# A two-layer decoder trunk in split fp32r: the tokens' high and low parts as one 512-column product

## The chip, the cores and the metric

The kernel runs on one core of a Trainium2 chip. The metric is the device time of one execution in microseconds. A kernel is timed in several runs and the median is given. One more execution is taken by the hardware profiler: it gives the page, the chain of waits and the timeline that are quoted here.

## The reference

Two pre-norm residual layers on 256 tokens of width 2048, all in float32. Layer a is multi-head latent attention, layer b block-sparse attention, which with 256 tokens is plain causal attention with ALiBi. Each has 16 heads of width 128, and a gate path that multiplies what the mixer gives before the output projection.

```
def moba_mixer(h, w_in, q_norm, k_norm):
    q, k, v, gate = jnp.split(h @ w_in, 4, axis=-1)
    q = rms_norm(to_heads(q, N_HEADS, HEAD_DIM), q_norm)
    k = rms_norm(to_heads(k, N_HEADS, HEAD_DIM), k_norm)
    v = to_heads(v, N_HEADS, HEAD_DIM)
    o = moba_attention(q, k, v, alibi_slopes())
    return from_heads(o) * jax.nn.silu(gate)

def reference(x, ...):
    for i in range(DEPTH):                       # DEPTH = 2
        if i == 0: y = mla_mixer(rms_norm(x, norm_a[0]), ...) @ w_out_a[0]
        if i == 1: y = moba_mixer(rms_norm(x, norm_b[0]), ...) @ w_out_b[0]
        x = x + y
    return x
```

In layer b, w_in is 2048 x 8192 (q, k, v and gate, 2048 columns each), w_out is 2048 x 2048.

## The kernel before

**Split products.** float32 data is cut into a high part in fp32r and a low part (what is left of it, again fp32r), and a product is the sum of three: high x high, high x low, low x high. Tokens are held with the features on the partitions: xh and xl are [128, 16, 256] (16 row blocks of 128 features, 256 tokens), ogh and ogl the same for the gated outputs of the 16 heads.

**Weights.** A weight piece is 128 x 1024 values (512 KB): SyncE's queue loads it (wr, four buffers, L132), ACT casts its high part (wh, four buffers, L146) and DVE subtracts to make the low part (wl, three buffers, L150). `run` issues these ahead of the step that uses the piece. A buffer is free again when TensorE is done with its piece.

**Blocks.** `blk_rows` has the weights stream as 512 moving columns against the tokens (q, k and v). `blk_cols` has the tokens stream as 256 moving columns against 128 weight columns, three products of 256 columns for each row block and each 128 weight columns (gates and output blocks). Two such 256-column results share a PSUM bank, five banks hold accumulators (`acc`).

**Order.** Each block is a list of steps, one for each row block. `ordered` sets one order of all steps by hand-written costs and lags: main steps in their list's order, side steps (attention heads, token scales) where their inputs are reckoned to be ready. TensorE's instructions are chained in that order. The other engines take their rows in an order of their own, fixed when the program is built.

**A head** has three side steps (`head_steps`): s1 makes the scores in PSUM (ps_s) and the softmax (sm: minimum on DVE, exp on ACT, normalising on DVE); s2 turns the probabilities by a DMA transpose, with a DVE copy out to pz in front (L407), the transpose issued by SyncE (L408) and a DVE copy back behind it (L409), and cuts them into ph (ACT), pl (DVE) and p1; s3 makes the product with v (ps_o), multiplies by the gate (og) and splits into ogh and ogl. Output block steps need the ogh and ogl of their head: step 12 that of head 12, and so on.

**Layer b** goes in four groups of four heads. A group is its gate block, q, k and v; the heads of a group run under the next group's gate, those of the last group under the first output blocks (`outs_b`). `gate_done` multiplies a gate by the token scale rows (rr) and applies tanh; `token_scale` makes these rows from ps_st and ps_r.

Of the kernel before, what the change touches and what calls it, by code (L numbers as in the profile page):

```python
# [21 lines left out]
F32R = mybir.dt.float32r  # L22
# [4 lines left out]
ALU = mybir.AluOpType  # L27

P = 128
S = 256  # L30
DM = 2048
NC = DM // P
H = 16
# [43 lines left out]
def paired(v):  # L77

    return v.rearrange("p (g l e) -> p g e l", l=2, e=16)


def lines(v):

    return v.rearrange("p (g l e) -> p g l e", l=2, e=16)


def unpaired(v):

    return v.rearrange("p (g e l) -> p g l e", l=2, e=16)
# [3 lines left out]
def trunk(ctx: ExitStack, tc, xT, gains, cst, w_in_a, w_q_up, w_kv_up, w_out_a, w_in_b, w_out_b, outT):  # L93
    nc = tc.nc
    pool = lambda name, **kw: ctx.enter_context(tc.tile_pool(name=name, **kw))
    one = pool("one", bufs=1)
# [5 lines left out]
    def acc(name):  # L102
        return pacc.tile([P, 512], F32, tag="acc", name=name)
# [86 lines left out]
    def chain(ins):  # L190

        if pe:
            tc.add_manual_dep(ins.ins, pe[-1].name, mybir.DependencyInfo(
                mybir.DependencyClass.NoSync, mybir.DependencyReason.DATA), reason="order")
        pe.append(ins.ins)

    def matmul(*args, **kw):
        chain(nc.tensor.matmul(*args, skip_group_check=True, **kw))  # L198
# [4 lines left out]
    def blk_rows(w, x, done, lag=PB, first=()):  # L203

        nk, n = w.shape[0] // P, w.shape[1]
        a = []

        def go(wt, c, k):
            xh, xl = x()
            if k == 0:  # L210
                a.extend(acc("acc") for _ in range(2))
            for t in range(2):
                ts = slice(t * P, (t + 1) * P)
                o = a[t][:, :n]
                matmul(o, xh[:, k, ts], paired(wt.h[:, c]), start=k == 0, stop=False)
                matmul(o, xh[:, k, ts], paired(wt.l[:, c]), start=False, stop=False)
                matmul(o, xl[:, k, ts], paired(wt.h[:, c]), start=False, stop=k == nk - 1)
            if k == nk - 1:
                done([a[t][:, :n] for t in range(2)])

        return _steps(w, go, 6 * (n / 2.4 + 2.5), lag, first, True)

    def blk_cols(w, x, done, lag=3000):

        nk, ns = w.shape[0] // P, w.shape[1] // P
        a = []

        def go(wt, c, k):
            xh, xl = x()
            if k == 0:  # L230
                a.extend(acc("acc") for _ in range(ns // 2))
            for s in range(ns):
                o = a[s // 2][:, (s % 2) * S:(s % 2 + 1) * S]
                ws = slice(s * P, (s + 1) * P)
                first = k == 0 and s % 2 == 0
                last = k == nk - 1
                matmul(o, wt.h[:, c, ws], paired(xh[:, k]), start=first, stop=False)
                matmul(o, wt.h[:, c, ws], paired(xl[:, k]), start=False, stop=False)
                matmul(o, wt.l[:, c, ws], paired(xh[:, k]), start=False, stop=last)
            if k == nk - 1:  # L240
                done(a)

        return _steps(w, go, 3 * ns * 109, lag)

    def _steps(w, go, cost, lag, first=(), moving=False):
        out, nc_w = [], 1024 // w.shape[1]
        nk = w.shape[0] // P
        k1 = 0
        for n in list(first) + [nc_w] * nk:
            k0, k1 = k1, min(k1 + n, nk)  # L250
            if k0 == nk:
                break
            wt = W(w[k0 * P:k1 * P], moving)
            for k in range(k0, k1):
                out.append(Step(lambda wt=wt, c=k - k0, k=k: go(wt, c, k), cost, lag if k == nk - 1 else 0,
                                w=wt if k == k0 else None))
        return out
# [26 lines left out]
    def big(dtype=F32):  # L284
        return one.tile([P, NC, S], dtype, tag="xt", name="xt")

    res["x"] = big()
    xh = one.tile([P, NC, S], F32R, name="xh")
    xl = one.tile([P, NC, S], F32R, name="xl")
    ogh = one.tile([P, H, S], F32R, name="ogh")  # L290
    ogl = one.tile([P, H, S], F32R, name="ogl")
    ident = c_sb[:, C_ID:C_ID + P]
    ones = one.tile([P, P], F32, name="ones")
    nc.vector.memset(ones, 1.0)
# [16 lines left out]
    def split_x(c, gcol):  # L311
        xt = res["x"]
        res["split"] = nc.scalar.activation(xh[:, c], xt[:, c], AF.Copy, scale=col(gcol + c))
        nc.vector.scalar_tensor_tensor(xl[:, c], xt[:, c], col(gcol + c), xh[:, c].bitcast(F32),
                                       op0=ALU.mult, op1=ALU.subtract)
# [6 lines left out]
    def sum_squares(ssq, j):  # L322

        xt = res["x"]
        sq = wk.tile([P, 2, S], F32, tag="gx", name="sq")
        after(nc.scalar.activation(sq, xt[:, 2 * j:2 * j + 2], AF.Square), res["split"])
        if j == 0:
            nc.vector.tensor_tensor(ssq, sq[:, 0], sq[:, 1], op=ALU.add)
        else:
            nc.vector.tensor_tensor(ssq, ssq, sq[:, 0], op=ALU.add)  # L330
            nc.vector.tensor_tensor(ssq, ssq, sq[:, 1], op=ALU.add)
# [26 lines left out]

    gate_of = {}

    def gate_done(g, rows):
        def done(a):
            for b in range(len(a)):
                ub = wk.tile([P, 2, S], F32, tag="gate", name="gate", bufs=4)
                gate_of[g + b] = ub
                x = wk.tile([P, 2, S], F32, tag="gx", name="gx")
                nc.vector.tensor_tensor(x, a[b].rearrange("p (h t) -> p h t", h=2),
                                        rows().unsqueeze(1).to_broadcast([P, 2, S]), op=ALU.mult)
                nc.scalar.activation(ub, x, AF.Tanh, scale=0.5)
                nc.vector.scalar_tensor_tensor(ub, ub, 1.0, x, op0=ALU.add, op1=ALU.mult)  # L370
        return done


    def products(ps, q, k, first):
# [87 lines left out]
    main, side = [], []  # L462
# [122 lines left out]
                transpose(ps[:, i * S + t * P:i * S + (t + 1) * P], src.rearrange("p a b -> p (a b)"), ident)  # L585
        parts(ps, 1.0, krf, *lat_st["kr"], True)

    x_a = lambda: (xh, xl)
    rows_a = lambda: scale_a["rows"]
    lat0 = blk_rows(w_in_a[:, 0:LAT // 2], x_a, lat_acc.append, 0, (1, 1))  # L590
    lat1 = blk_rows(w_in_a[:, LAT // 2:LAT], x_a, lat_acc.append, 0)
# [123 lines left out]
    def out_done_a(j):  # L715
        def f(a):
            xt = res["x"]
            c = 2 * j
            both = lines(xt[:, c:c + 2].rearrange("p a b -> p (a b)"))
            nc.vector.tensor_tensor(both, unpaired(a[0]), both, op=ALU.add)  # L720
            split_x(c, G_NB)
            split_x(c + 1, G_NB)
            sum_squares(ssq_b, j)
        return f
# [5 lines left out]
    ssq_b = one.tile([P, S], F32, tag="ssq", name="ssq")  # L730
    scale_b = {}
    rx2 = one.tile([P, 2], F32, name="rx2")
    og = lambda: (ogh, ogl)
    outs_a = [blk_cols(w_out_a[:, 256 * j:256 * (j + 1)], og, out_done_a(j), 4000) for j in range(8)]

    for g in range(8):
        main += group_a(g)
# [20 lines left out]
    x_b = x_a  # L758
    rows_b = lambda: scale_b["rows"]

    def group_b(g):
        z = {}
# [59 lines left out]
            return f  # L822

        w = lambda i: w_in_b[:, DM * i + 512 * g:DM * i + 512 * (g + 1)]
        gate = blk_cols(w(3), x_b, gate_done(2 * g, rows_b))
        q = blk_rows(w(0), x_b, n_done("q"))
        k = blk_rows(w(1), x_b, n_done("k"))
        v = blk_rows(w(2), x_b, v_done, 3000)
        old = hb[4 * g - 8:4 * g - 4] if g > 1 else []
        last = [h[0] for h in hb[-4:]] if g else [h[0] for h in heads[-4:]]  # L830
        tq = Step(turn("q", gq_b), 0, TUB, q[-1:], last)
        tk = Step(turn("k", col(G_KB)), 0, TUB, k[-1:], last)
        for h in range(4):
            hb.append(head_steps(4 * g + h, scores(h), bias(4 * g + h), lambda h=h: [x[:, h] for x in z["v"]],
                                 545, [tq, tk], v[-1:] + gate[-1:], [], S2B, nc.vector.tensor_copy))
        gate[-1].after += [h[2] for h in old] + [row_b]
        v[-1].after += [h[2] for h in old]
        if g:
            q[-1].after += turns_of[-2]
            k[-1].after += turns_of[-1]  # L840
        else:
            for i, s in enumerate(gate):
                s.needs.append(outs_a[i // 2][-1])
        turns_of.extend([[tq], [tk]])
        side.extend([tq, tk])
        side.extend(s for h in hb[-4:] for s in h)
# [2 lines left out]
    def out_done_b(j):  # L849
        def f(a):  # L850
            xt = res["x"]
            for b in range(2):
                c = 4 * j + 2 * b
                y = xt[:, c:c + 2]
                both = lines(y.rearrange("p a b -> p (a b)"))
                nc.vector.tensor_tensor(both, unpaired(a[b]), both, op=ALU.add)  # L856
                nc.sync.dma_start(outT[c * P:(c + 2) * P].rearrange("(c p) t -> p c t", p=P), y)
        return f

    outs_b = [blk_cols(w_out_b[:, 512 * j:512 * (j + 1)], og, out_done_b(j)) for j in range(4)]  # L860

    col_b, row_b = token_scale(ssq_b, "b", scale_b, [outs_a[7][-1]], scales_b)
    side += [col_b, row_b]
    hb = []
    for g in range(4):
        main += group_b(g)
    for b in outs_b:
        for i, s in enumerate(b):
            s.needs.append(hb[i][2])
    main += outs_b[0][:12] + outs_b[1][:6] + outs_b[0][12:] + outs_b[1][6:] + outs_b[2] + outs_b[3]  # L870
    run(ordered(main, side))


# [59 lines left out]
```

## Time and profile before

| | us |
|---|---|
| median of 3 runs | 759.71 (758.45 to 760.53) |
| profiled execution, whole time | 760.14 |
| its span | 758.0 |
| TensorE busy in it | 746.2 (98%) |
| weight loads busy | 708.0 (93%) |
| DVE busy | 576.2 (76%) |
| ACT busy | 488.3 (64%) |

PE is TensorE's products, PEld its weight loads, DVE the vector engine, ACT the scalar engine, SPq the queue of SyncE, which issues the DMAs. A product's recorded duration contains its way through the array, so products overlap in the records; the pace is read from their starts. "x12" is a count of instructions.

### The profile page before, as it was taken

The page shows a single profiled execution, that of the slowest core. Times are in us where ns is not written, and L with a number is a line of the kernel's source. Part 1 is how long each engine was busy: PE and PEld are TensorE (multiplying, and loading weights), DVE is VectorE, ACT ScalarE, POOL GpSimd, SP SyncE. Part 2 cuts the span into 40 slices and gives each one's busy share as a digit, 9 for nine tenths or more (in the row PEclk, how much of TensorE's full clock was granted, in tenths as well). Part 3 has the DMA queues.
Part 4 walks back from the last instruction along what each step waited for, and adds up shares of the span by engine and source line. Part 5 has one row for each costly group of instructions (what it writes and reads, how often), then busy time and mean ns, then how long its engine had stood idle before and what let it go on. Part 6 is the DMA issues. An engine that isn't in the chain of part 4 may idle for free.

```text
span 758.0 us, 14123 instructions
## 1 busy us (share of the span) xinstructions
PE 746.2 (98%) x5246; PEld 708.0 (93%) x5246; DVE 576.2 (76%) x1207; ACT 488.3 (64%) x1025; POOL 0.2 (0%) x4
## 2 busy tenths in 40 slices
PE   8999999999999899999999999999999999999997
PEld 7999999999999899998889988998889988899997
DVE  6888899898997585765888767886688857887552
ACT  7767888888877464545667566665567666574431
POOL 0000000000000000000000000000000000000000
PEclk9999999999999999999999999999999999999999
DMA  9866665666557966667886778876788778867771
GB/s 304 257 177 180 185 177 167 181 156 185 162 167 222 248 195 199 196 189 202 228 234 174 200 221 229 229 188 208 188 240 230 188 211 220 231 181 215 250 223 44
DMA packets 137973, 153.19 MB, mean 202 GB/s; under 512 B 47280, under 2 KB 94768, under 8 KB 137904
## 3 DMA queue, kind: packets, MB, share of 16 engines
q1 hardware_dynamic: 137760, 152.27, 70.7%
q8 instruction: 41, 0.67, 0.4%
q14 instruction: 28, 0.23, 0.1%
q10 hardware_dynamic: 144, 0.02, 0.0%
HBM read 139.68 MB, written 2.10 MB: 187 GB/s over the span
## 4 chain that ended last, share of the span: by engine, by line
PE 66%; DMA 1%; ACT 0%; DVE 0%; issue 0%; SPq 0%
PE acc L198 63%; PE ps_o L198 1%; PE ps_s L198 1%; DMA sm<-pz 1%; ACT wh L146 0%; DVE xt L856 0%; DVE pz L409 0%; PE ps_r L198 0%; PE ps_st L198 0%; ACT alibi L819 0%; SPq L408 0%; DVE pl L440 0%; ACT pz L407 0%; ACT ogh L455 0%; ACT sm L426 0%
## 5 line engine op out<-in xcount | busy, mean ns | idle before, releaser
L146 ACT ACTIVATE wh<-wr 128x1024 fp32r<-128x1024 f32 (+3 forms) x265 | 288.0, 1091 | 161.3 <-PE acc L198 144.0
L150 DVE TENSOR_TENSOR wl<-wr,wh 128x1024 fp32r<-128x1024 f32 (+3 forms) x265 | 313.9, 1187 | 90.6 <-PE acc L198 59.1
L198 PE MATMUL acc<-wh,xh 128*128 128x512 f32 (+1 forms) x448 | 168.6, 376 | 1.4 <-ACT wh L146 1.4
L198 PE MATMUL acc<-wl,xh 128*128 128x512 f32 (+1 forms) x448 | 167.5, 374 | 1.0 <-DVE wl L150 1.0
L198 PE MATMUL acc<-wh,xl 128*128 128x512 f32 (+1 forms) x448 | 167.2, 373 | 0.0
L198 PE MATMUL acc<-ogh,wh 128*128 128x256 f32 x512 | 142.7, 279 | 0.0
L198 PE MATMUL acc<-xh,wh 128*128 128x256 f32 x512 | 142.4, 278 | 0.0
L198 PE MATMUL acc<-ogl,wh 128*128 128x256 f32 x512 | 141.7, 277 | 0.0
L198 PE MATMUL acc<-ogh,wl 128*128 128x256 f32 x512 | 141.6, 276 | 0.0
L198 PE MATMUL acc<-xh,wl 128*128 128x256 f32 x512 | 140.8, 275 | 0.0
L198 PE MATMUL acc<-xl,wh 128*128 128x256 f32 x512 | 140.8, 275 | 0.0
L198 PEld LDWEIGHTS acc<-ogh,wl 128*128 128x128 f32 x512 | 99.1, 194 | 0.0
L198 PEld LDWEIGHTS acc<-ogl,wh 128*128 128x128 f32 x512 | 99.0, 193 | 0.1
L198 PEld LDWEIGHTS acc<-ogh,wh 128*128 128x128 f32 x512 | 99.0, 193 | 0.0
L198 PEld LDWEIGHTS acc<-xl,wh 128*128 128x128 f32 x512 | 98.2, 192 | 0.3
L198 PEld LDWEIGHTS acc<-xh,wh 128*128 128x128 f32 x512 | 98.2, 192 | 0.3
L198 PEld LDWEIGHTS acc<-xh,wl 128*128 128x128 f32 x512 | 98.3, 192 | 0.0
L198 PEld LDWEIGHTS acc<-wh,xh 128*128 128x128 f32 x448 | 84.7, 189 | 12.1 <-ACT wh L146 2.0
L198 PEld LDWEIGHTS acc<-wl,xh 128*128 128x128 f32 x448 | 84.7, 189 | 11.7 <-DVE wl L150 1.7
L198 PEld LDWEIGHTS acc<-wh,xl 128*128 128x128 f32 x448 | 84.7, 189 | 10.3
L198 PE MATMUL acc<-wh,xt 128*128 128x384 f32 (+1 forms) x192 | 57.5, 357 | 0.0
L409 DVE COPY pz<-sm 128x768 uint16<-128x768 uint16 x32 | 19.4, 605 | 22.7 <-DMA sm<-pz 22.4
(154 smaller groups left out, 841.1 us busy)
## 6 DMA issues: line engine op xcount, KB each, us to landing
wr<-w_in_b SPq DMA_DIRECT2D x128, 512.0 KB, 4.3
wr<-w_in_a SPq DMA_DIRECT2D x32, 512.0 KB, 4.0
wr<-w_out_a SPq DMA_DIRECT2D x32, 512.0 KB, 4.0
wr<-w_out_b SPq DMA_DIRECT2D x32, 512.0 KB, 4.6
wr<-w_in_a SPq DMA_DIRECT2D x15, 416.0 KB, 5.3
wr<-w_q_up SPq DMA_DIRECT2D x16, 384.0 KB, 3.8
wr<-w_kv_up SPq DMA_DIRECT2D x8, 512.0 KB, 3.8
xt<-xT SPq DMA_DIRECT2D x4, 512.0 KB, 5.7
```

Of the source, the lines that this page charges most:

```text
L146: nc.scalar.activation(self.ordering(self.h)[1], self.ordering(self.raw)[0], AF.Copy)
L150: nc.vector.tensor_tensor(self.ordering(self.l)[1], self.ordering(self.raw)[0], self.ordering(self.h.bitcast(F32))[1], op=ALU.subtract)
L198: chain(nc.tensor.matmul(*args, skip_group_check=True, **kw))
L409: nc.vector.tensor_copy(words(b), planes(a))
```

## The change

Where it applies, high and low tokens lie side by side in one tile (xhl, ohl: [128, 16, 512]). The high weights then meet both in one product of 512 columns, which fills a PSUM bank; the low weights meet the high tokens in a product of 256 columns that adds into the bank's first half. The two halves are added at the end: in a gate by an ACT copy of the second half and a DVE addition, in an output block by two additions to the residual instead of one. It applies to layer b's gates, to output blocks 4 to 7 of layer a and 0 to 6 of layer b. A block of 256 weight columns now takes two banks where it took one. Layer b's gates become two blocks of 256 weight columns where there was one of 512, its output blocks eight of 256 where there were four of 512, and 24 of their steps stand ahead of the first that needs the last group's heads, where 18 (of twice the width) stood.

```
+    def blk_both(w, x, done, lag=3000):
+        nk, ns = w.shape[0] // P, w.shape[1] // P
+        a = []
+        def go(wt, c, k):
+            hl = x()[2]
+            if k == 0:
+                a.extend(acc("acc") for _ in range(ns))
+            for s in range(ns):
+                ws = slice(s * P, (s + 1) * P)
+                last = k == nk - 1
+                matmul(a[s], wt.h[:, c, ws], paired(hl[:, k]), start=k == 0, stop=last)
+                matmul(a[s][:, :S], wt.l[:, c, ws], paired(hl[:, k, :S]), start=False, stop=last)
+            if k == nk - 1:
+                done(a)
+        return _steps(w, go, ns * 326, lag)
...
+    xhl = one.tile([P, NC, 2 * S], F32R, name="xhl")
+    ohl = one.tile([P, H, 2 * S], F32R, name="ohl")
+    xh, xl, ogh, ogl = xhl[:, :, :S], xhl[:, :, S:], ohl[:, :, :S], ohl[:, :, S:]
...
+                if halves:
+                    y = x
+                    for h in range(2):
+                        z = a[2 * b + h]
+                        nc.scalar.copy(x[:, h], z[:, S:])
+                        nc.vector.tensor_tensor(x[:, h], z[:, :S], x[:, h], op=ALU.add)
...
+    def added(a, xt, c):
+        both = xt[:, c:c + 2].rearrange("p a b -> p (a b)")
+        ys = [both] if len(a) == 1 else [xt[:, c], xt[:, c + 1]]
+        n = 2 * S // len(a)
+        for o in range(0, 2 * S, n):
+            for y, b in zip(ys, a):
+                nc.vector.tensor_tensor(lines(y), unpaired(b[:, o:o + n]), lines(y), op=ALU.add)
...
+    outs_a = [(blk_cols if j < 4 else blk_both)(w_out_a[:, 256 * j:256 * (j + 1)], og, out_done_a(j), 4000) for j in range(8)]
...
-        gate = blk_cols(w(3), x_b, gate_done(2 * g, rows_b))
+        gate = []
+        for i in range(2 * g, 2 * g + 2):
+            gate += blk_both(w_in_b[:, 3 * DM + 256 * i:3 * DM + 256 * (i + 1)], x_b, gate_done(i, rows_b, True))
...
-    outs_b = [blk_cols(w_out_b[:, 512 * j:512 * (j + 1)], og, out_done_b(j)) for j in range(4)]
+    outs_b = [(blk_both if j < 7 else blk_cols)(w_out_b[:, 256 * j:256 * (j + 1)], og, out_done_b(j)) for j in range(8)]
...
-    main += outs_b[0][:12] + outs_b[1][:6] + outs_b[0][12:] + outs_b[1][6:] + outs_b[2] + outs_b[3]
+    main += outs_b[0][:12] + outs_b[1][:12] + outs_b[0][12:] + outs_b[1][12:] + sum(outs_b[2:], [])
```

**DVE, under the gate of layer b's second group.** Before, this is what DVE does from the copies out of the third and fourth head (pz_5526, pz_5548; sm is the probabilities, og the gated output, gx the gate):

```order
L407 COPY pz_5526<-sm_5399 128x768
L407 COPY pz_5548<-sm_5435 128x768
L150 TENSOR_TENSOR wl_5562<-wr_5508,wh_5510 128x1024
L409 COPY pz_5526<-sm_5399 128x2x384
L150 TENSOR_TENSOR wl_5592<-wr_5558,wh_5560 128x1024
L409 COPY pz_5548<-sm_5435 128x2x384
L150 TENSOR_TENSOR wl_5622<-wr_5588,wh_5590 128x1024
L454 SCALAR_TENSOR_TENSOR og_5641<-ps_o_5636,gate_4736 128x256
L440 TENSOR_TENSOR pl_5531<-pz_5526,ph_5530 128x256
```

Now, in the same place, from the gate's first addition on (pz_5276 is the second head's, pz_5300 the third's, pz_5347 the fourth's; wl_5331 and wl_5365 are the gate's seventh and eighth weight piece, wl_5387 the first of q):

```order
L392 TENSOR_TENSOR gx_5319<-acc_5132,gx_5319 128x256
L443 COPY pz_5276<-sm_5175 128x2x384
L392 TENSOR_TENSOR gx_5319<-acc_5133,gx_5319 128x256
L150 TENSOR_TENSOR wl_5331<-wr_5286,wh_5288 128x1024
L474 TENSOR_TENSOR pl_5281<-pz_5276,ph_5280 128x256
L393 TENSOR_TENSOR gx_5319<-gx_5319,rr_b_4464 128x512
L443 COPY pz_5300<-sm_5203 128x2x384
L441 COPY pz_5347<-sm_5243 128x768
L395 SCALAR_TENSOR_TENSOR gate_5318<-gate_5318,gx_5319 128x512
L150 TENSOR_TENSOR wl_5365<-wr_5327,wh_5329 128x1024
L150 TENSOR_TENSOR wl_5387<-wr_5361,wh_5363 128x1024
L443 COPY pz_5347<-sm_5243 128x2x384
```

The second head's copy back used to be done before the last two copies out, and the eighth piece (wl_5562) came ahead of the third head's copy back; now the seventh stands behind the second head's copy back, and the eighth behind the third's and the gate's multiplications.

**DVE, in the tail of layer b**, where the last four heads run under output blocks 0 and 1. Before, from the copies out of the third and fourth head (pz_8370, pz_8392):

```order
L407 COPY pz_8370<-sm_8243 128x768
L407 COPY pz_8392<-sm_8279 128x768
L150 TENSOR_TENSOR wl_8406<-wr_8352,wh_8354 128x1024
L409 COPY pz_8370<-sm_8243 128x2x384
L150 TENSOR_TENSOR wl_8436<-wr_8402,wh_8404 128x1024
L409 COPY pz_8392<-sm_8279 128x2x384
L150 TENSOR_TENSOR wl_8468<-wr_8432,wh_8434 128x1024
L454 SCALAR_TENSOR_TENSOR og_8487<-ps_o_8482,gate_7553 128x256
L440 TENSOR_TENSOR pl_8375<-pz_8370,ph_8374 128x256
```

Now, from the copy out of the third head (pz_7984; pz_7958 is the second's, pz_8020 the fourth's):

```order
L441 COPY pz_7984<-sm_7885 128x768
L465 TENSOR_SCALAR sm_7925<-sm_7925,ri_7932 128x128
L465 TENSOR_SCALAR sm_7925<-sm_7925,ri_7932 128x256
L150 TENSOR_TENSOR wl_8006<-wr_7968,wh_7970 128x1024
L443 COPY pz_7958<-sm_7857 128x2x384
L474 TENSOR_TENSOR pl_7963<-pz_7958,ph_7962 128x256
L150 TENSOR_TENSOR wl_8038<-wr_8002,wh_8004 128x1024
L443 COPY pz_7984<-sm_7885 128x2x384
L441 COPY pz_8020<-sm_7925 128x768
L150 TENSOR_TENSOR wl_8087<-wr_8034,wh_8036 128x1024
L488 SCALAR_TENSOR_TENSOR og_8061<-ps_o_8056,gate_7106 128x256
L474 TENSOR_TENSOR pl_7989<-pz_7984,ph_7988 128x256
```

The fourth head's copy out used to follow the third's at once; it now comes behind the copies back of the second and third.

**TensorE, in the tail**, at the third head's output product now (before, 12 products of an output block stood between the first two ps_o and 24 ahead of the third):

```order
L198 MATMUL ps_o_8065<-p1_7966,v1_7804 128x128
L198 MATMUL ps_o_8074<-ph_7988,vh_7802 128x256
L198 MATMUL ps_o_8074<-pl_7989,vh_7802 128x256
L198 MATMUL ps_o_8074<-ph_7988,vl_7803 128x256
L198 MATMUL ps_o_8074<-p1_7992,v1_7804 128x128
L198 MATMUL acc_7814<-ohl_74,wh_7970 128x512
L198 MATMUL acc_7814<-ohl_74,wl_8006 128x256
L198 MATMUL acc_7815<-ohl_74,wh_7970 128x512
L198 MATMUL acc_7815<-ohl_74,wl_8006 128x256
L198 MATMUL ps_o_8093<-ph_8024,vh_7802 128x256
```

The first three ps_o stand one behind the other, and one output step of four products stands ahead of the fourth.

## Rows read from the trace of the kernel before

**Rows 1.** The page's head: span, and busy time of each engine.
```profile
span 758.0 us, 14123 instructions
PE 746.2 (98%) x5246; PEld 708.0 (93%) x5246; DVE 576.2 (76%) x1207; ACT 488.3 (64%) x1025; POOL 0.2 (0%) x4
```

**Rows 2.** The chain that ended last, in order: start, duration, what.
```profile
258.07 60.97 PE acc L198 x546
...
319.48 8.04 PE acc L198 x72
...
400.94 0.58 PE ps_s L198 x5
...
420.68 0.61 PE ps_o L198 x5
...
425.82 0.60 PE ps_o L198 x5
...
428.33 60.95 PE acc L198 x294
...
665.96 0.58 PE ps_s L198 x5
...
690.93 0.61 PE ps_o L198 x5
...
753.32 1.36 DVE xt L856 x2
```

**Rows 3.** Groups by line and form: busy us, mean ns, idle before.
```profile
L150 DVE TENSOR_TENSOR wl<-wr,wh 128x1024 fp32r<-128x1024 f32 x232 | 282.4, 1220 | 86.6 <-PE acc L198 59.1 <-issue 19.6 <-ACT wh L146 4.6
...
L639 DVE TENSOR_TENSOR tok<-acc,rs_y 128x256 f32<-128x256 f32 x32 | 11.9, 412 | 0.0
...
L856 DVE TENSOR_TENSOR xt<-acc,xt 128x512 f32<-128x512 f32 x8 | 5.4, 690 | 7.5 <-PE acc L198 7.5
...
L625 ACT COPY v<-acc 128x256 f32<-128x256 f32 x8 | 3.1, 392 | 0.0
```

**Rows 4.** DVE's timeline under the second group's gate: start, duration, row.
```profile
404.75 0.56 DVE L407 COPY pz<-sm 128x768 uint16<-128x768 uint16 x1
...
409.01 0.61 DVE L409 COPY pz<-sm 128x768 uint16<-128x768 uint16 x1 [1.02 <-DMA sm<-pz]
...
414.66 1.02 DVE L407 COPY pz<-sm 128x768 uint16<-128x768 uint16 x2
415.60 1.22 DVE L150 TENSOR_TENSOR wl<-wr,wh 128x1024 fp32r<-128x1024 f32 x1
420.42 0.61 DVE L409 COPY pz<-sm 128x768 uint16<-128x768 uint16 x1 [3.61 <-DMA sm<-pz]
420.92 1.21 DVE L150 TENSOR_TENSOR wl<-wr,wh 128x1024 fp32r<-128x1024 f32 x1
...
424.01 0.41 DVE L440 TENSOR_TENSOR pl<-pz,ph 128x256 fp32r<-128x256 f32 x1
```

**Rows 5.** DMA transposes issued at 404 to 407 and 413 to 416 us: us to landing.
```profile
sm<-pz SPq DMA_TRANSPOSE x1, 3.7
...
sm<-pz SPq DMA_TRANSPOSE x1, 5.1
...
415.24 2.62 SPq L408 DMA_TRANSPOSE sm<-pz  x2
```

**Rows 6.** A wait of TensorE under layer a's output blocks: timeline, chain, granted clock.
```profile
251.88 0.38 PE L198 MATMUL ps_o<-ph,vh 128*128 128x256 f32 x1 [2.67 <-ACT ph L439]
...
253.16 4.30 PE acc L198 x24
...
254.00:258.00 4.00, 4.00 (x25) 4.00 (x24) 3.21 (x4) 2.63 (x4) 0.00 (x0) 0.64 1.09 342
```

More of the change, by code (lines that the diff above doesn't have):

```diff
@@ L208, in go @@
         def go(wt, c, k):
-            xh, xl = x()
+            xh, xl = x()[:2]
             if k == 0:
@@ L228, in go @@
         def go(wt, c, k):
-            xh, xl = x()
+            xh, xl = x()[:2]
             if k == 0:
@@ L287, in trunk @@
     res["x"] = big()
[L288 to L291, printed above, removed]
+    xhl = one.tile([P, NC, 2 * S], F32R, name="xhl")
+    ohl = one.tile([P, H, 2 * S], F32R, name="ohl")
+    xh, xl, ogh, ogl = xhl[:, :, :S], xhl[:, :, S:], ohl[:, :, :S], ohl[:, :, S:]
     ident = c_sb[:, C_ID:C_ID + P]
@@ L359, in trunk, with gate_done @@
     gate_of = {}
-    def gate_done(g, rows):
+    def gate_done(g, rows, halves=False):
         def done(a):
-            for b in range(len(a)):
+            for b in range(len(a) // 2 if halves else len(a)):
                 ub = wk.tile([P, 2, S], F32, tag="gate", name="gate", bufs=4)
@@ L366, in done @@
                 x = wk.tile([P, 2, S], F32, tag="gx", name="gx")
-                nc.vector.tensor_tensor(x, a[b].rearrange("p (h t) -> p h t", h=2),
-                                        rows().unsqueeze(1).to_broadcast([P, 2, S]), op=ALU.mult)
+                y = a[b].rearrange("p (h t) -> p h t", h=2)
+                if halves:
[4 more added lines that the diff above has]
+                        nc.vector.tensor_tensor(x[:, h], z[:, :S], x[:, h], op=ALU.add)
+                nc.vector.tensor_tensor(x, y, rows().unsqueeze(1).to_broadcast([P, 2, S]), op=ALU.mult)
                 nc.scalar.activation(ub, x, AF.Tanh, scale=0.5)
@@ L586, in kr_t @@
         parts(ps, 1.0, krf, *lat_st["kr"], True)
-    x_a = lambda: (xh, xl)
+    x_a = lambda: (xh, xl, xhl)
     rows_a = lambda: scale_a["rows"]
@@ L718, in f @@
             c = 2 * j
-            both = lines(xt[:, c:c + 2].rearrange("p a b -> p (a b)"))
-            nc.vector.tensor_tensor(both, unpaired(a[0]), both, op=ALU.add)
+            added(a, xt, c)
             split_x(c, G_NB)
@@ L732, in trunk @@
     rx2 = one.tile([P, 2], F32, name="rx2")
-    og = lambda: (ogh, ogl)
-    outs_a = [blk_cols(w_out_a[:, 256 * j:256 * (j + 1)], og, out_done_a(j), 4000) for j in range(8)]
+    og = lambda: (ogh, ogl, ohl)
+    outs_a = [(blk_cols if j < 4 else blk_both)(w_out_a[:, 256 * j:256 * (j + 1)], og, out_done_a(j), 4000) for j in range(8)]
     for g in range(8):
@@ L835, in group_b @@
                                  545, [tq, tk], v[-1:] + gate[-1:], [], S2B, nc.vector.tensor_copy))
-        gate[-1].after += [h[2] for h in old] + [row_b]
+        for s in (gate[NC - 1], gate[-1]):
+            s.after += [h[2] for h in old] + [row_b]
         v[-1].after += [h[2] for h in old]
@@ L842, in group_b @@
             for i, s in enumerate(gate):
-                s.needs.append(outs_a[i // 2][-1])
+                s.needs.append(outs_a[i % NC // 2][-1])
         turns_of.extend([[tq], [tk]])
@@ L851, in f @@
             xt = res["x"]
[L852 to L857, printed above, removed]
+            c = 2 * j
+            added(a, xt, c)
+            nc.sync.dma_start(outT[c * P:(c + 2) * P].rearrange("(c p) t -> p c t", p=P), xt[:, c:c + 2])
         return f
-    outs_b = [blk_cols(w_out_b[:, 512 * j:512 * (j + 1)], og, out_done_b(j)) for j in range(4)]
+    outs_b = [(blk_both if j < 7 else blk_cols)(w_out_b[:, 256 * j:256 * (j + 1)], og, out_done_b(j)) for j in range(8)]
     col_b, row_b = token_scale(ssq_b, "b", scale_b, [outs_a[7][-1]], scales_b)
```

## The prediction

> **What bounds the kernel now.** The page comes first: TensorE is busy for 98% of the span, and its weight loads for nearly as much [rows 1]. A busy TensorE is not yet a full one, so the chain of waits comes next, in order of time: from 253 us to the end it is TensorE's products, one after the other, with no wait of any size in it [rows 2]. A change therefore pays what it takes out of TensorE's stream, and costs whatever makes TensorE wait. The pace is in the chain too. In the output blocks 546 products of 256 columns took 60.97 us, 111.7 ns each. A later piece holds 24 of these and 270 of 512 columns: 60.95 less 2.68 is 58.27 us, 215.8 ns each [rows 2]. So 256 columns cost more than half of 512. The reader is then to see in DVE's timeline how close the other work stands: it is busy 76% [rows 1], takes its rows in the program's order, and waits inside that order for the DMA transposes [rows 4].
>
> **The products.** There are 608 places (a row block times 128 weight columns) that change: 4 x 64 in the gates, 4 x 32 in w_out_a, 7 x 32 in w_out_b. Three products of 256 columns (335.0 ns) become one of 512 and one of 256: 215.8 + 111.7 = 327.5. That is 7.5 ns, **4.6 us** in all. No row shows the two kinds alternating. From above: were the 256 columns as cheap as half of a 512, 107.9 ns, the pair would take 323.7 and the gain be 6.9. From below: a pair as long as the three, nothing. I take the paces as they stand, since both kinds run beside their weight loads in the trace.
>
> The Trainium skill ("TensorE: Matmul & The Clock Gate", section "Back-to-back issue gap") gives a warm gap of N / 2.4 + 2.5 ns. The row for 512 columns agrees (215.8); the row for 256 (111.7) does not (109.2). By the page a pair saves one fixed 2.5 ns, an estimate of 1.5 us in all, and my sum would come out 3.1 us higher.
>
> **The end.** The last output block is 256 columns wide where it was 512, so one addition is left behind the last product instead of two: 1.36 [rows 2] against 0.69 [rows 3], **0.7 us** less.
>
> **The new work beside TensorE.** Each of 16 gate banks gets an ACT copy (0.39, by the copy of the same size) and a DVE addition (0.41): 6.3 and 6.6 us. Each of 11 output blocks has four additions of 0.41 for one of 0.69, 10.5 us of DVE [rows 3]. TensorE's 750 us would hide all of it if it stood in the gaps. What follows is about where it stands.
>
> **Where DVE's order makes TensorE wait.** Heads of a layer-b group are called H1 to H4. Each goes ps_s, softmax, copy out (L407), DMA transpose, copy back (L409), pl, ps_o. In DVE's timeline a row ends about 0.1 after the next begins (420.42 + 0.61 against 420.92), so I count 1.13 for a wl, 0.5 for a copy back, 0.47 for a copy out (two: 1.02), 0.33 for 256 and 0.6 for 512 columns [rows 3, 4]. A transpose lands 3.7 or 5.1 after its issue [rows 5]; I take 3.6 to 3.7, since in the new order none stands right behind another, as those at 415.24 do.
>
> Before, counted from H1's ps_s at 400.94 [rows 2]: the gate's eighth weight piece is cast at 14.7 (415.60) and needed at 18.4; DVE then waits 3.61 for a transpose, which hurts nobody; pl of H3 ends at 424.42, 1.4 ahead of its ps_o at 425.82 [rows 2, 4]. That is the cover that there is.
>
> After, from H1's ps_s = 0 again. The order puts 4, 4, 16 and 80 gate products between the four ps_s (0.58 each) and the first ps_o: ps_s at 0, 1.24, 2.47, 5.67, ps_o at 19.3, 20.6, 21.9. A piece serves 8 pairs, 2.62 us; the seventh starts at 16.07, the eighth at 18.7, and its wl is needed with the second product, 0.22 later. On DVE:
> - H1's copy out starts at 4.4 (3.8 before [rows 2, 4]; ACT now makes a wh between the two exps), its copy back at 8.7. Only after H3's normalising, H4's minimum and pl of H1 comes H2's copy out, at 10.6, where it stood ahead of H1's copy back. Its transpose is issued at 11.1 and lands at 14.7.
> - All that stands behind this copy back waits: copy back to 15.2, the gate's second addition to 15.55, wl of the seventh piece to 16.75. TensorE wants it at 16.29: **0.5**.
> - pl, gate product, H3's copy back, H4's copy out and the gate's last product (0.33 + 0.6 + 0.5 + 0.47 + 0.6) to 19.15, wl of the eighth piece to 20.4, wanted at 18.7 + 0.5 + 0.22: **1.0**.
> - H4's transpose is issued at 18.6 and copied back from 22.3; a wl to 23.95, og, and pl of H3 at 24.65. Its ps_o, due at 21.9 + 1.5 + 0.1, waits **1.2**.
>
> On SyncE's queue each of these transposes has a weight load ahead of it, which waits for a wl of the piece four before; these end at 7.5, 12.1 and 16.75, before the copies out, so the queue holds none up. 2.7 for each of three groups: **8.1 us**. With every landing at 5.1 the same sum gives 5.6 a group.
>
> **The tail.** The fourth group's heads run under the first output blocks of layer b. Before, 24.1 us of products need none of them (12 steps of 12 products and 6 more); after, 24 steps of 0.65, 15.7. H1's ps_s to H3's ps_o was 24.97 [rows 2] and is now 17.3, three ps_o back to back. DVE's chain is the same up to H2's copy back at 14.7; then pl (ph first) to 15.95, wl to 17.1, H3's copy back to 17.6, H4's copy out to 18.05, wl to 19.2, og, pl of H3 to 19.85: TensorE waits 2.5. H4's transpose is issued at 18.1, lands at 21.7, and pl of H4 ends at 23.3: ps_o, due at 21.2, waits 2.1. Together **4.6**. In the trace a wait of 2.67 was followed by 24 products in 4.30 us for 2.68, at a granted clock of 0.64 over 4 us, so part of it at 1.2 GHz [rows 6]. I add **1.6**. With landings at 5.1 the waits are 7.6.
>
> **The change from layer a to b.** The row of token scales now stands 7 steps of 0.65 (4.6 us) behind its statistics, where it stood 8.0 [rows 2]. Twelve short dependent DVE operations and two wl lie between: late by about **0.4**. At each change of block the four additions (1.4) stand ahead of the second piece's wl, which ends at 2.8 with 2.84 to go: **0.3** over ten of them, 3 if the additions are as long as they look.
>
> **Sum.** The profiled execution's time is 760.14 (span 758.0 and 2.1 around it). 760.1 - 4.6 - 0.7 + 8.1 + 4.6 + 1.6 + 0.4 + 0.3 = 769.8. That execution lies 0.4 above the median of 759.71, so **769.4**, slower by 1.3%. With 1.5 to 4 a group and 3 to 8 in the tail, this case spans 763 to 775.
>
> **Rivals.**
> - *TensorE never waits* (ends faster): only the products and the end count, 754.4. For it: DVE has a quarter of the time free, and the DMA lands early in many places. Against: the wl stands behind the transposed copy in a fixed order. It decides if H2's transpose lands before about 13 (1.6 earlier than I have it) and H4's, in the tail, before 17.5. 0.17.
> - *Only the tail waits*: the groups' eighth piece comes in time, 754.4 + 4.6, with the clock 1.6 more: 759.0 to 760.6. For it: a group has 80 products of cover against 60 in the tail. 0.10.
> - *The transposes land at 5.1*, as those at 415.24 do: 16.8 + 7.6 + 1.6 of waits, 781. Against: fewer stand back to back. 0.11.
> - *The pair saves little or nothing*, because a weight load behind 512 columns doesn't hide as well as I take it to: up to 774. Against: both paces [rows 2] come from streams with a load for each product. 0.05. By the page named above it would be 772.5.
>
> **Chances.** The forecast has 0.57. A measurement of this kernel tells 0.3% (2.3 us) from nothing. Slower: 0.57 + 0.11 + 0.05 = 0.73; same: 0.09 of the tail case; faster: 0.17 and what is left, 0.18. The range 756 to 777 leaves out most of the first rival and part of the third, about 0.2.
>
> **What would show it.** Right: TensorE's chain has 512- and 256-column products alternating at some 327 ns a pair; it breaks three times for DVE's wl or pl in each of the groups whose ps_s stand at about 400, 488 and 577 us, and for 4 to 5 us before the last two ps_o of the tail, with a lowered clock behind them; TensorE's busy time falls by about 4.6 where nothing waits. Wrong: no idle time of TensorE before wl, ph or pl; H2's copy back long before 14.7 from its ps_s; or a pair at 335 ns.

## The result and the profile after

The changed kernel takes 768.11 us (median of 6 runs, 765.5 to 770.26) against 759.08 for the kernel before beside it (6 runs, 757.72 to 760.53): a ratio of 1.0121, 95% interval 1.0104 to 1.0138. It is slower by 1.2%, inside the range and 1.3 us from the forecast. The profiled execution is the slowest of the six, 770.26. That time hides errors of both signs among its terms, and the runs below tell them apart.

The head of the changed kernel's page, against [rows 1]:

```profile
span 768.5 us, 12960 instructions
...
PE 750.1 (98%) x4638; PEld 692.4 (90%) x4638; DVE 592.7 (77%) x1256; ACT 493.5 (64%) x1041; POOL 0.2 (0%) x4
```

There are 608 products fewer, and TensorE is busy 3.9 us longer, though its shorter stream should have taken 4.6 off: products at a lower clock count as busy for longer. So the busy share tells nothing here, and the waits come next. TensorE's waits after 300 us (us in total, times, longest), where the kernel before has none:

```profile
PE acc L198 <- DVE wl L150: 2.1, 2, 1.6
PE ps_o L198 <- DVE pl L474: 1.9, 4, 1.3
PE ps_o L198 <- ACT ph L473: 1.6, 2, 1.4
PE ps_r L198 <- DVE diag L369: 0.5, 1, 0.5
```

The chain of the changed kernel (start, length, what), where [rows 2] had TensorE's products alone:

```profile
261.92 59.50 PE acc L198 x400
...
327.32 0.81 PE ps_r L198 x2
...
403.39 0.58 PE ps_s L198 x5
...
421.60 2.22 DVE wl L150 x2
...
425.91 0.34 DVE pl L474
...
426.29 0.76 PE ps_o L198 x4
...
492.44 0.58 PE ps_s L198 x5
...
581.05 0.58 PE ps_s L198 x5
...
671.31 0.58 PE ps_s L198 x5
...
674.36 2.62 PE acc L198 x16
...
688.68 4.30 DMA sm<-pz
...
694.17 1.68 PE ps_o L198 x5
695.86 68.71 PE acc L198 x444
764.59 0.69 DVE xt L405
```

The chain now leaves TensorE for transposes, casts and a pl in each of the three groups, and for a transpose with its copy back and ph in the tail. How large is the loss? From one group's first ps_s to the next, the kernel before takes 88.34 each time (400.94 to 489.28 in its chain); with 64 pairs that save 7.5 ns it should be 87.86. The changed kernel takes 89.05, 88.61 and 90.26: losses of 1.2, 0.8 and 2.4, **4.3** in all. From the last group's first ps_s to the end of the span, before takes 92.0 (665.96 to 758.0). The changed kernel has 0.7 us of output products there that stood ahead of it, 224 pairs (1.7) and the shorter end (0.7): 90.4 without waits. It takes 97.2 (671.31 to 768.5), a loss of **6.8**.

The table of waits shows less than these sums. TensorE's timeline says why (start, length, in brackets the idle time and what ended it), first pairs without a wait in an output block of layer a, then a wait for a cast in the first group:

```profile
290.21 0.38 PE L198 MATMUL acc<-ohl,wh 128*128 128x512 f32 x1
290.43 0.27 PE L198 MATMUL acc<-ohl,wl 128*128 128x256 f32 x1
290.54 0.38 PE L198 MATMUL acc<-ohl,wh 128*128 128x512 f32 x1
...
421.92 0.38 PE L198 MATMUL acc<-xhl,wh 128*128 128x512 f32 x1
422.79 0.38 PE L198 MATMUL acc<-xhl,wl 128*128 128x256 f32 x1 [0.48 <-DVE wl L150]
423.00 0.38 PE L198 MATMUL acc<-xhl,wh 128*128 128x512 f32 x1
```

The 256-column product starts 0.22 behind the 512 one when nothing is late, and 0.87 behind it when the cast is: 0.65 lost, with 0.48 shown. A product's recorded end lies some 0.16 past the point where the next could have started, so a wait costs about that much more than its row says.

### The profile page after: what moved, and what is told of

Read it like the earlier page. It is cut to its first block, busy times and chain, and to the rows that moved or that the text cites. A ratio compares the mean times of both kernels' runs of the same rounds, so it can differ in the third digit from the quotient of the medians.

```text
span 768.5 us, 12960 instructions
## 1 busy us (share of the span) xinstructions
PE 750.1 (98%) x4638; PEld 692.4 (90%) x4638; DVE 592.7 (77%) x1256; ACT 493.5 (64%) x1041; POOL 0.2 (0%) x4
## 4 chain that ended last, share of the span: by engine, by line
PE 56%; DVE 5%; DMA 5%; ACT 1%; issue 1%; DVEq 0%; ACTq 0%
PE acc L198 54%; DMA sm<-pz 5%; DVE wl L150 2%; PE ps_o L198 1%; DVE pz L441 1%; ACT sm L460 1%; PE ps_s L198 1%; DVE pz L443 0%; DVE sm L465 0%; ACT wh L146 0%; DVE pl L474 0%; DVE sm L458 0%; DVE gate L395 0%; DVE og L488 0%; ACT ph L473 0%
## 5 line engine op out<-in xcount | busy, mean ns | idle before, releaser
L198 PE MATMUL acc<-wh,xhl 128*128 128x512 f32 (+1 forms) x896 | 265.0, 376 | 1.9 <-ACT wh L146 1.9
L198 PEld LDWEIGHTS acc<-wh,xhl 128*128 128x128 f32 x896 | 169.7, 190 | 23.0 <-ACT wh L146 2.4
L198 PE MATMUL acc<-xhl,wh 128*128 128x256 f32 (+1 forms) x768 | 174.7, 314 | 0.0
L198 PE MATMUL acc<-ohl,wh 128*128 128x512 f32 (+1 forms) x672 | 174.7, 338 | 0.0
L198 PE MATMUL acc<-wl,xhl 128*128 128x512 f32 (+1 forms) x448 | 168.3, 376 | 0.9 <-DVE wl L150 0.8
L198 PE MATMUL acc<-xhl,wl 128*128 128x256 f32 x512 | 140.6, 275 | 2.2 <-DVE wl L150 2.1
L198 PE MATMUL acc<-ohl,wl 128*128 128x256 f32 x512 | 141.7, 277 | 0.0
L198 PEld LDWEIGHTS acc<-xhl,wh 128*128 128x128 f32 x768 | 126.3, 191 | 6.3
L198 PEld LDWEIGHTS acc<-ohl,wh 128*128 128x128 f32 x672 | 117.9, 195 | 9.5
L198 PEld LDWEIGHTS acc<-ohl,wl 128*128 128x128 f32 x512 | 100.1, 195 | 0.0
L443 DVE COPY pz<-sm 128x768 uint16<-128x768 uint16 x32 | 19.5, 609 | 14.0 <-DMA sm<-pz 13.9
L473 ACT CAST ph<-pz 128x256 fp32r<-128x256 f32 x32 | 12.9, 404 | 24.4 <-DVE pz L443 22.9
```

The costliest lines, as they stand in the source:

```text
L443: nc.vector.tensor_copy(words(b), planes(a))
L473: nc.scalar.copy(ph, pz[:, :S])
```

## The experiments

Every kernel has the same code up to layer a's output blocks, and its traces start these between 256.05 and 261.92 us, without regard to what was changed later (the changed kernel once at 261.92 and once at 257.36). So the table gives, beside the measured ratio to the kernel before, the stretch from that point to the end of the span, the three groups' loss and the tail's, worked out as above (parts without pairs against 88.34 or 92.0; where the gates alone have pairs, the third group holds 0.7 of output products more, which is taken off; with a third output block ahead, one block fewer has pairs, and the tail without waits is 90.6). The last three columns come from one profiled execution each, and it need not be the middle one: with both outputs and the third block, and with DVE's order and the third block, it is the fastest of twelve; with DVE's order alone the slowest of six; without the sum the second slowest of twelve.

| kernel | ratio (95%) | stretch, us | groups | tail |
|---|---|---|---|---|
| before | 1 | 499.9 | 0 | 0 |
| changed | 1.0121 (1.0104 to 1.0138) | 506.6 | 4.3 | 6.8 |
| changed, once more | 1.012 (1.0089 to 1.0151) | 507.8 | 4.3 | 8.1 |
| layout only | 0.9993 (0.9976 to 1.0011) | 499.75 | 0 | 0 |
| layer a's outputs only | 0.9976 (0.9961 to 0.9992) | 498.7 | 0 | 0 |
| gates only | 1.0035 (1.0022 to 1.0048) | 502.7 | 4.2 | 0 |
| layer b's outputs only | 1.0053 (1.0032 to 1.0074) | 505.6 | 0 | 8.0 |
| gates, no sum | 1.0026 (1.0007 to 1.0045) | 503.0 | 4.4 | 0 |
| changed, third block ahead | 1.0073 (1.0048 to 1.0099) | 503.4 | 4.5 | 3.2 |
| both outputs, third block ahead | 1.0026 (1.0004 to 1.0047) | 499.3 | 0 | 2.4 |
| changed, DVE's order | 1.0059 (1.004 to 1.0079) | 504.95 | 2.5 | 7.0 |
| the same and third block ahead | 0.9989 (0.9974 to 1.0004) | 498.3 | 1.2 | 1.4 |
| gates only, DVE's order | 1.0002 (0.9987 to 1.0018) | 500.35 | 1.7 | 0 |
| before, DVE's order | 1.0003 (0.9982 to 1.0025) | 499.75 | 0 | 0 |

**One part at a time.** The four kernels put the tiles, and then one group of blocks, into the kernel before.

```
+    xhl = one.tile([P, NC, 2 * S], F32R, name="xhl")         # all four
+    outs_a: (blk_cols if j < 4 else blk_both)                # layer a's outputs
+    gate: two blk_both of 256 columns, gate_done(..., True)  # gates
+    outs_b: (blk_both if j < 7 else blk_cols), new main      # layer b's outputs
```

> Only the tiles change: the high and low parts of the tokens lie beside each other in one tile (xhl, and ohl for the gated outputs), and every block streams three products of 256 columns as before. My theory (pairs save, and the order of DVE's work makes TensorE wait in layer b): nothing here changes that, so 0 against the kernel before, within 1 us. Rival (the layout itself is slower to write or read; the changed kernel's trace was already 2.6 to 3.9 us late at its second hundred to 260 us, in code that the change leaves alone): 2.5 to 4 us slower.

> The layout, and the last four output blocks of layer a as pairs; gates and layer b's output blocks as before. My theory: 128 places by 7.5 ns, 1.0 us faster than the kernel before, no new wait of TensorE. Rival of the layout: 1.5 to 3 us slower. Rival that a pair saves nothing: 0.

> The layout, and layer b's gates as pairs in blocks of 256 columns with their halves added; output blocks as before. Pairs give 256 x 7.5 ns = 1.9 us back. By the changed kernel's trace the first three groups then lose 4.3 us in waits for DVE (8.1 by the prediction) and the row of token scales 0.5: 2.9 us slower than the kernel before (6.7 by the prediction). The fourth group's heads run under the old output blocks with their 24 us of cover, so no wait there. Rival of the layout: 5 to 7 us slower, with the early part late. Rival that these waits come with the output blocks alone: 1.9 us faster.

> The layout, and layer b's output blocks as pairs of 256 columns wide with their new order (24 steps of 0.65 us ahead of the heads instead of 18 that give 24.1 us); gates and layer a's blocks as before. Pairs give 224 x 7.5 ns = 1.7 us, the narrower end 0.7. The tail's waits of 5.4 and the products slowed by the clock behind them 1.0 go against it: 4.0 us slower than the kernel before, all of it from 660 us on. Rival of the layout: 6.5 to 8 us slower. Rival that the tail's wait needs the gate's additions on DVE too: 2.4 us faster.

The layout costs nothing. The 128 pairs in layer a shorten the stretch by 1.0 against the layout alone, 8 ns each: the products' term stands, and the median is 1.5 us lower. The gates lose 4.2 in waits for 1.9 won, the output blocks 8.0 for 2.4: each of these two is slower by itself, and neither needs the other. Against the layout alone the three stretches add up to -1.0 + 2.9 + 5.8 = 7.7; the changed kernel's two executions show 6.8 and 8.1.

**Once more, unaltered.**

> The changed kernel once more, unaltered. Its parts measured alone came to -1.5, +3.3 and +4.9 us by their medians, 6.8 together, and from 260 us to the end its trace lost 6.65 us; but its median stood 9.0 above that of before, and its trace was 3.85 us late by 260 us. If the parts add up and the late start was this execution's: 5 to 7.5 us slower, and its trace no later at 260 us than that of before. Rival (the parts together do something that none does alone): 9 us slower, late at 260 us again.

It started layer a's outputs at 257.36, not late, with a stretch of 507.8. So the late start belonged to one execution. In that one the granted clock was 0.91 in the first 20 us, where before and the repeat have 1.00, and 0.85 between 240 and 260, where they have 0.91. The ratio is the same, 1.012, and I take the parts as adding up.

**Less work on DVE.** Each half is scaled straight from its bank: one 256-column operation for an addition and half of a scaling, and no ACT copy.

```
-                        nc.scalar.copy(x[:, h], z[:, S:])
-                        nc.vector.tensor_tensor(x[:, h], z[:, :S], x[:, h], op=ALU.add)
-                nc.vector.tensor_tensor(x, y, rows().unsqueeze(1).to_broadcast([P, 2, S]), op=ALU.mult)
+                        nc.vector.tensor_tensor(x[:, h], z[:, :S], rows(), op=ALU.mult)
+                else:
+                    nc.vector.tensor_tensor(x, y, rows().unsqueeze(1).to_broadcast([P, 2, S]), op=ALU.mult)
```

> The gates as pairs, as in the run of the gates alone, but ACT copies no half and DVE adds none: the product of the gate's weights with the tokens' low part is left out of the result (TensorE still makes it), and DVE scales each half straight from its bank. Each gate bank so has about 0.8 us less of DVE in front of the casts. My theory (TensorE waits since DVE's casts stand behind late transposes, so part of the wait is order and part is work): the gates' waits of 3.0 us halve, so 1 to 2 us faster than the gates alone. Rival (all of the wait is the added work): no wait of TensorE in the groups, 3 us faster, 1.9 us faster than before after the row of scales. Rival (it is all order): no change.

TensorE's waits after 300 us in that kernel:

```profile
PE ps_o L198 <- DVE pl L474: 2.2, 3, 0.8
PE acc L198 <- DVE wl L150: 0.9, 1, 0.9
PE ps_r L198 <- DVE diag L369: 0.5, 1, 0.5
```

In the trace my theory missed: the wait moved from the cast to pl, and the groups' loss stayed, 4.4 for 4.2. The times are less clear. By the ratios this kernel is some 0.7 us faster than the gates alone, by the medians 1.8 (1.5 above before's, against 3.4), and the intervals overlap; executions with a mean granted clock of 1.0 took 760.55 to 761.99 here (seven) and 761.34 and 762.23 with the sums. So the rival that all of the wait is the added work is out, and whether a small part of it is stays open.

**More products ahead of the tail's heads.**

```
-    outs_b = [(blk_both if j < 7 else blk_cols)(w_out_b[:, 256 * j:256 * (j + 1)], og, out_done_b(j)) for j in range(8)]
+    outs_b = [(blk_cols if j in (2, 7) else blk_both)(w_out_b[:, 256 * j:256 * (j + 1)], og, out_done_b(j)) for j in range(8)]
...
-    main += outs_b[0][:12] + outs_b[1][:12] + outs_b[0][12:] + ...
+    main += outs_b[0][:12] + outs_b[1][:12] + outs_b[2][:12] + outs_b[0][12:] + ...
```

> The changed kernel, with the first 12 steps of a third output block of layer b ahead of the fourth group's heads. That block streams three products into one bank, since two blocks of pairs take four of the five banks. 12 steps of 0.67 us are 8.0 us more of products that need no head; the block gives back 32 x 7.5 ns = 0.24. My theory (too few products stood between the tail's heads): the tail's waits of 5.4 and the clock's 1.0 go, about 6 us faster than the changed kernel, 1 to 3 us slower than before; no wait before the ps_o after 670 us. Rival (DVE's order is the cause and holds the tail up wherever the products stand): the waits stay, within 2 us of the changed kernel.

> The gates as before; pairs in the last four blocks of layer a and in six blocks of layer b (not in the third and the last), with the 12 further steps ahead of the heads. If each part acts by itself: 128 + 192 places by 7.5 ns, 2.4 us, and 0.7 at the end, so 3.1 us faster than before (ratio 0.996), and no wait of TensorE after 300 us. Rival (the narrower blocks make the tail wait whatever stands ahead): 759 us or more.

The waits were expected to go, and in both kernels a part of the tail's loss stays: 3.2 of 6.8, and 2.4 of 8.0. The chain of the first in the tail:

```profile
688.21 4.57 DMA sm<-pz
692.87 0.09 DVE pz L443
...
693.36 1.21 DVE wl L150
694.57 0.34 DVE og L488
694.90 0.34 DVE pl L474
695.29 0.76 PE ps_o L198 x4
```

The longer cover changed DVE's order as well: H3's pl (L474) now stands behind H4's copy back (L443), as it does in the groups. In the changed kernel H3's pl was done 19.1 us after the first ps_s (690.45 against 671.31), here after 24.6, so TensorE waits 2.6 at that ps_o in spite of 8 us more to do (1.8 in the second kernel). So neither theory had it alone: the cover helps, and the order takes a part of it back. The second kernel should have beaten the one before and did not: its executions run from 758.88 at a mean granted clock of 0.997, the profiled one, to 764.89 at 0.991.

**Another order on DVE, the same on TensorE.** A head's copy out and copy back become two steps, and a copy back may not stand ahead of the next head's copy out. TensorE's instructions stand in the order of the changed kernel.

```
-        b = Step(s2, 0, lag, [a])
+            b1 = Step(s2a, 0, FRONT, [a])      # copy out, DMA transpose
+            b = Step(s2b, 0, BACK, [b1])       # copy back, ph, pl
+                hb_b[-1][0].after.append(b1)   # the head before: its copy back after this copy out
```

> The changed kernel with TensorE's order word for word the same; only DVE's order in layer b differs. A head's copy out with its transpose, and its copy back, are two steps, and the copy back of one head may not stand ahead of the copy out of the next. My theory (TensorE waits since DVE stands at a copy back for a transpose that was issued just before, with casts and the next copy out behind it): the three groups' waits of 4.3 us go, and of the tail's 6.8 some 2 to 3 stay, since its heads have 16 us of products; 7 to 8 us faster than the changed kernel, within 2 us of before, and no wait in the groups. Rival (too little other work of TensorE between a group's heads, whatever DVE's order): 5 to 9 us slower than before, as the changed kernel. Rival (the additional DVE and ACT work): the same.

> The gates alone as pairs, with that order of DVE; output blocks as before. My theory: the gates' waits go but for the row of scales: 1.9 less 0.5, 1.4 us faster than before, some 4.5 faster than the gates alone. Rival (the waits come of the added work or of too few products): 2.5 to 3.5 us slower than before, as the gates alone.

> The layout with three products a place everywhere, as the kernel before, with that order of DVE. A control: TensorE had no wait in layer b, so the order has nothing to give back: 0 within 1 us. Rival (the order by itself makes the kernel faster, so that the runs with pairs would owe their gain to it): 1.5 us faster or more.

> That order of DVE, and a third output block ahead of the fourth group's heads (its first 12 steps, three products a place into one bank). My theory: no wait of TensorE after 300 us but the one for the row of token scales, 0.5. Then the pairs give 576 x 7.5 ns = 4.3 us and the end 0.7, less 0.5 and up to 0.3 at the changes of block: 3.5 to 4.5 us faster than before (ratio 0.994 to 0.9955), faster than both kernels. Rival (transposes that land at 4.5 still hold up the tail, as with the third block alone): a wait of about 2 us stays, 1.5 to 2.5 faster than before. Rival (something else of the pairs costs time): before's time or more.

With DVE's order alone the groups' loss falls from 4.3 to 2.5, and no cast is late any more; the waits after 300 us:

```profile
PE ps_o L198 <- ACT ph L496: 2.3, 3, 1.6
PE ps_o L198 <- DVE pl L497: 0.7, 1, 0.7
PE ps_r L198 <- DVE diag L371: 0.5, 1, 0.5
```

What is left is a new wait, for the fourth head. The chain of that kernel in the second group:

```profile
507.98 0.03 DVEq L150
...
508.12 5.52 DMA sm<-pz
513.65 0.62 DVE pz L483
...
514.81 0.44 DVE pl L497
...
515.29 0.76 PE ps_o L198 x4
```

H4's copy out stands behind a cast, three weight loads had been issued just ahead of its transpose, and it landed after 5.5. The control shows that the order alone gives nothing, so what it gives here is the waits'. The median is 3.6 us above before's, where I had expected 2 at most; the changed kernel's are 9.0 and 7.5 above. The tail did not follow my expectation: its loss stays at 7.0, and H3's copy back now stands behind H4's copy out there. Only with the third block ahead as well does it fall, to 1.4. That kernel has all the pairs but one block's, takes 757.96 (before: 759.67), 1.7 us less where I had expected 3.5 to 4.5, and beats the changed kernel; against the kernel before, its interval holds 1. The gates alone with that order come out even, where I had expected 1.4 us.

## Why the prediction was right

**The pair.** Eight pairs take 2.62 us in the changed kernel, 327.5 ns each, the sum of the two paces as forecast. The Trainium skill's rule that the prediction weighed against it ("TensorE: Matmul & The Clock Gate", section "Back-to-back issue gap", which gives it for a product on its own) makes a pair 325.0 and its saving 2.5 ns, an estimate. The trace decides otherwise: the pair takes 327.5, and layer a's pairs alone saved 8 ns each. The end shrank from 1.36 to 0.69 as said. The rival of a pair that saves nothing is out.

**The groups: right mechanism, size too large.** Forecast 8.1, measured 4.3. The term that was mis-sized is the landing of a transpose, taken as 3.6 to 3.7 for every one, since none was to stand right behind another. The SyncE queue's issues in the changed kernel's first group, and one of the third, and then DVE's rows:

```profile
408.11 1.23 SPq L442 DMA_TRANSPOSE sm<-pz  x1
...
413.52 1.22 SPq L442 DMA_TRANSPOSE sm<-pz  x1
...
415.42 1.22 SPq L442 DMA_TRANSPOSE sm<-pz  x1
...
585.77 1.22 SPq L442 DMA_TRANSPOSE sm<-pz  x1
```

```profile
411.10 0.61 DVE L443 COPY pz<-sm 128x768 uint16<-128x768 uint16 x1 [0.26 <-DMA sm<-pz]
...
412.94 0.55 DVE L441 COPY pz<-sm 128x768 uint16<-128x768 uint16 x1
...
416.30 0.61 DVE L443 COPY pz<-sm 128x768 uint16<-128x768 uint16 x1 [0.34 <-DMA sm<-pz]
...
417.12 1.21 DVE L150 TENSOR_TENSOR wl<-wr,wh 128x1024 fp32r<-128x1024 f32 x1
...
419.95 0.62 DVE L443 COPY pz<-sm 128x768 uint16<-128x768 uint16 x1 [0.67 <-DMA sm<-pz]
...
589.87 0.61 DVE L443 COPY pz<-sm 128x768 uint16<-128x768 uint16 x1 [1.37 <-DMA sm<-pz]
```

The order is the one forecast: H2's copy out behind H1's copy back and H2's copy back ahead of the seventh piece's cast. But the first two landed after 3.0 and 2.8, so H2's copy back came 12.9 after the first ps_s, not 14.7, and the seventh piece in time. H3's, issued 1.9 behind H2's, took 4.5: here the premise fails that none stands right behind another. DVE waits 0.67 for it, and the eighth piece's cast behind it is what TensorE waits for at 422.79. So the waits are in the order forecast, but in this group it is H3's transpose that sets them and not H2's. In the third group H1's took 4.1 and H3's 4.6; there the loss is 2.4 against a forecast of 2.7. The groups were also right in what they are not: not the layout, and at most in small part the added work.

**The tail: right in sum, by luck.** Forecast 4.6 of waits and 1.6 for the clock, measured 6.8. H3's pl came 1.6 late, H4's ph 1.4, with 0.4 ahead of H3; the rest goes with the clock. H4's transpose was issued 0.7 earlier than forecast (17.4 after the first ps_s) and took 4.3, and so it landed at 21.7 as forecast. Windows of the changed kernel (PE, PEld, DVE, ACT, POOL, granted clock, DMA share, GB/s):

```profile
690.00:694.00 4.00, 2.31 (x8) 1.61 (x8) 2.11 (x7) 1.16 (x3) 0.00 (x0) 0.62 1.10 225
694.00:698.00 4.00, 3.83 (x14) 3.36 (x15) 1.85 (x5) 1.14 (x4) 0.00 (x0) 0.53 0.01 2
698.00:720.00 22.00, 22.00 (x137) 20.23 (x136) 13.91 (x21) 8.77 (x9) 0.00 (x0) 1.00 0.65 204
```

At 0.53, nearly all of it at 1.2 GHz, TensorE starts 14 products in 4 us where it starts 137 in 22 afterwards (some 25 in 4). So waits of about 3.4 were followed by as much again: the clock's term was too small by half, the waits' too large, and the two errors cancelled.

**The rest.** The row of token scales came 0.5 late (forecast 0.4). From layer a's outputs to the first ps_s the changed kernel's chain takes 141.47 against 142.87: 192 pairs give 1.4, 0.7 of products moved across, 0.5 was lost at ps_r, so about 0.2 is left for the changes of block (forecast 0.3 in all).

**The sum.** Forecast +9.7 and, by the same terms, measured -4.6 - 0.7 + 4.3 + 6.8 + 0.5 + 0.3 = 6.6 in the profiled execution (7.9 by its repeat's stretch). The other 3.85 of the 10.5 between the two profiled spans is the late start, which no term had and which the repeat did not show. The medians are 9.0 and 7.5 apart, where 9.7 was forecast. That the forecast came within 1.3 us of the time is luck in part: its terms came 1.8 to 3.1 us too high, and the first median lies 1.1 to 2.4 us above what the terms give. In the changed kernel's twelve executions the mean granted clock was 0.988 to 0.995, in those of before beside the experiments 0.993 to 1.0, most often 0.998 or 1.0; that may be the rest, and no run separates it. The rivals: transposes at 5.1 would have needed 781; only the tail waiting is refuted by the gates alone; TensorE never waiting needed H2's transpose at 13, and it landed at 12.9, yet losses of 0.8 and more stayed in the groups, since H3's took 4.3 to 4.6 and not the 3.7 that it was counted with.

**Shown and not shown.** Shown: the gates and layer b's output blocks each make TensorE wait by themselves; the waits are not the layout, and not the sums alone; with TensorE's order fixed, DVE's order takes away between two fifths and three quarters of the groups' loss (4.3 to 2.5, 4.2 to 1.7, 4.5 to 1.2); more products ahead take away more than half of the tail's, and both together most of it. Not shown: why a transpose lands after 2.7 us in one place and 4 to 6 in another. In the changed kernel H3's, issued 1.9 behind H2's with a weight load between them, took 4.3 to 4.6 in all four places, and ten of the other twelve 2.7 to 3.0; no run takes apart what of this is the transpose ahead and what the load. Kernels with a third buffer for pz, or with the last head's copy out moved further ahead, weren't tried.

## What to carry to other kernels

When TensorE is the bound and its stream is shortened, list what runs in fixed order under that stretch, and see by how much the latest piece of it was early: here it was 1.4 us, and a saving of 4.6 spread over the kernel cost 11 in the places where that margin went. A wait costs more than its row: here some 0.2 us that the row leaves out, and in the tail a lower clock behind it that was worth as much as the wait. Test such a change part by part: the one part that had no dependent chain beneath it (layer a's blocks) was the only one that paid.

## What the runs showed of the hardware

- The clock behind a wait does not follow the wait's length alone. The last head of layer a waits for its ph in every kernel, and 24 products of 256 columns follow: 2.68 at full clock. After a wait of 2.1 they took 2.68 in three executions (layout, both kernels with one kind of output blocks); after 1.6 once 2.68 (gates with DVE's order) and once 4.13 (gates only); after 1.7 they took 3.94 (the repeat), after 1.9 twice 4.3 (before with DVE's order; both outputs with the third block), after 2.3 3.44 (gates, no sum); after 2.7 to 3.0, 4.30 or more. In the changed kernel's third group a wait of 1.6 left the granted clock at 1.00.
- A transpose of the same size (128 x 768 in 16-bit words) landed between 2.7 and 6.0 us after its issue in these traces. The prediction had rows for 3.7 and 5.1 only, and its chain was most sensitive to just that.
- Executions of the same kernel differ by some 6 us in 760 (the kernel before from 757.4 to 764.0 in one series), and the time goes with the mean granted clock: 29 executions of the kernel before at 1.0 took 757.3 to 759.9, 16 at 0.993 to 0.996 took 761.1 to 764.0. The profiled one need not be the middle one: the changed kernel's first trace was its slowest run of six.
